# Shared raw-weight ring, earlier squares, kept weights and earlier output weights in a two-branch decoder layer

## The chip, the cores and the metric

The kernel runs on one core of one Trainium2 chip. The metric is the device time of one execution in microseconds (us). The instructions of one profiled execution are known with their start, duration and waits; all views shown are of that execution.

## The reference

One decoder layer over 2048 tokens of width 1024, with 16 meta tokens ahead of them. A root-mean-square norm is followed by one projection to 6400 columns; two attention branches run on its parts; their outputs are gated, projected, merged and projected once more, and a final norm follows.

```python
xn = rms_norm(h, norm_gain[l])
proj = xn @ w_in[l]
sb_q, sb_k, sb_v, sw_q, sw_k, sw_v, sb_z, sw_z, g_sb, g_sw = jnp.split(proj, offsets, axis=-1)
o_sb = stick_breaking_attention(sb_q, sb_k, sb_v, valid)       # 8 heads of 64, all earlier keys
o_sw = sliding_window_sink_attention(rope(sw_q), rope(sw_k), sw_v, attn_sinks[l], valid)  # 16 heads, 2 kv heads, window 128
y_sb = (o_sb * jax.nn.silu(sb_z)) @ w_branch_sb[l]
y_sw = (o_sw * jax.nn.silu(sw_z)) @ w_branch_swa[l]
merged = jax.nn.sigmoid(g_sb) * y_sb + jax.nn.sigmoid(g_sw) * y_sw
h = h + merged @ w_out[l]
return rms_norm(h, final_norm_gain)[:, BLOCK:]
```

Stick-breaking attention takes, for each query, a running product over the keys behind it; sliding-window attention ("banded" below) is a softmax over a band of 128 keys and one learned sink logit per head.

## The kernel before

The 2048 tokens stand in reverse order and are worked on in four groups of 512 (g = 0 to 3), two groups at a time: half 0 takes groups 2 and 3, half 1 takes groups 0 and 1. Matrix products keep nearly full single precision by splitting each operand into a high and a low part and running three matmuls for one (lines 376 to 378, and 211 to 213 and 268 to 270 at the end).

**Stages.** The start loads x, computes the norm's scales of the first group (`scales`: 8 loads of 128 x 512, a Square with a running sum on ScalarE for each, then a logarithm and an exponential for the inverse root) and `prep` builds xh and xl, the normalised input in two parts. Then in each half: projections for stick-breaking and the sliding window with `window` and `attend` (banded attention, lines 543 to 721) woven between them; after that the gate projections with `stick` (lines 724 to 854) woven between them. `finish` (lines 191 to 312) runs the branch projections, the merge, the output projection and the final norm, again half by half.

**Order.** TensorE's instructions stand in the order in which the program writes them, and `weave` mixes the two streams of work by a cost ratio. The other engines' orders come from a scheduler that places every instruction by a simulated timeline: among instructions that are ready it takes the one earliest in the program, so loads are drawn far ahead of the place where they are written, and work of a later stage is put among that of an earlier one. Each engine then works strictly in that order. All transfers are issued on SyncE's queue (line 55), also in one order. Buffers come from rings: a tile of a tag waits until one of the tag's buffers is free.

**Weights.** `weights` (line 156) loads one column tile of 128 columns as `raw` (512 KB, two buffers), splits it into `wh` and `wl` (three buffers each; the high part on GpSimd or ScalarE, the low part on GpSimd or VectorE) and stores both parts to HBM. The next call for the same tile takes them from HBM and forgets that they are there: the entry of `kept` is popped. Most column tiles are asked for twice, once in each half. The eight query tiles of the sliding window (`sw_q`) are asked for four times, since each half asks once for each of its groups.

**Turned tiles of v.** For stick-breaking, `sb_v` takes differences of neighbouring rows of v, turns them by TensorE transposes into `ps_zm` (one bank) and evacuates them with a split into `vt` (one buffer, 512 KB), which is stored to HBM as `vd` (lines 475 to 481). Each projection of v gives two such tiles, one for each group, turned while the next projection tile runs.

**Scales of half 1.** `group_scales` for groups 0 and 1 is called in the stick-breaking stage of half 0, between the tenth and the eleventh of its gate tiles (line 915). The 16 squares and the two inverse roots are ScalarE work; the results are used by `prep` at the end of half 0 and the start of half 1.

**Output projection.** For each group and each pair of row tiles (t0, t0 + 1), `finish` runs four blocks of 24 matmuls: the left half-row (ch = 0) for both row tiles, then the right one (ch = 1). Behind each block, VectorE adds the residual tile `res` (line 272) and ScalarE squares the sum (line 276). The output weights of ch = 0 are split during the merge (line 252), and those of ch = 1 (eight loads into the ring "a" of six, a cast on ScalarE, line 222, and a subtraction on VectorE, line 223, each) behind the first two blocks (line 282).

Of the kernel before, what the change touches and what calls it, by code (L numbers as in the profile page):

```python
# [7 lines left out]
F32 = mybir.dt.float32  # L8
F32R = mybir.dt.float32r
# [7 lines left out]
P = 128  # L17
D = 1024
# [26 lines left out]
def tile_kernel(ctx, tc, x, xt, meta, metat, gain, w_in, w_sb, w_sw, w_out, sinks, fgain,  # L45
# [27 lines left out]
    def late_consts():  # L73
        for i in range(2):
            DMA(sel[:, i, :], sel_c)
        DMA(skb, sinks.to_broadcast([P, 16]))
# [79 lines left out]
    def weights(c0, w=w_in):  # L156

        n = w.shape[2]
        wh, wl = (wp.tile([P, KT, P], F32R, tag=t, name=t, bufs=3)[:, :n, :] for t in ("wh", "wl"))
        key = w.name, c0  # L160
        if key in kept:
            for t, k in zip((wh, wl), kept.pop(key)):
                DMA(t, k)
            return wh, wl
        raw = wp.tile([P, KT, P], F32, tag="raw", name="raw", bufs=2)[:, :n, :]
        DMA(raw, w[c0 // P])
        split(wh, wl, raw)
        kept[key] = [dram(f"{t}_{w.name}_{c0}", [P, n, P], F32R) for t in "hl"]
        for t, k in zip((wh, wl), kept[key]):
            DMA(k, t)  # L170
        return wh, wl
# [19 lines left out]
    def finish(ringl, osw, first):  # L191
# [23 lines left out]
        for half, groups in enumerate(halves):  # L215
            part, merged, wo = {}, {}, {}

            def out_weights(k, ch):
                raw = small("a", AB)
                DMA(raw, w_out[0, k * P:(k + 1) * P, ch * GT:(ch + 1) * GT])  # L220
                h, l = wo[k, ch] = ringr(), ringr()
                A.copy(h, raw)
                V.tensor_tensor(l, raw, f32(h), op=ALU.subtract)
# [29 lines left out]
            for g in groups:  # L253
                for t0 in range(0, 4, 2):
                    res, ssq = {}, {}
                    end = (half, g, t0) == (1, groups[1], 2)
                    for ch in range(2):
                        cs = slice(ch * GT, (ch + 1) * GT)
                        for t in (t0, t0 + 1):
                            row = g * GT + t * P  # L260
                            if ch == 0:
                                res[t] = cp.tile([P, D], F32, tag="xr", name="res", bufs=3)
                                DMA(res[t], x[row:row + P, :])
                            acc = bank()
                            ts = slice(t * P, (t + 1) * P)
                            for k in range(KT):
                                (mh, ml), (wh, wl) = merged[k, g], wo[k, ch]
                                T.matmul(acc, lhsT=mh[:, ts], rhs=wh, start=k == 0, stop=False)
                                T.matmul(acc, lhsT=mh[:, ts], rhs=wl, start=False, stop=False)
                                T.matmul(acc, lhsT=ml[:, ts], rhs=wh, start=False, stop=k == KT - 1)  # L270
                            r = res[t][:, cs]
                            V.tensor_tensor(r, acc, r, op=ALU.add)
                            sq = cp.tile([P, GT], mybir.dt.bfloat16, tag="a", name="sq", bufs=AB)
                            if ch == 0:
                                ssq[t] = cp.tile([P, 2], F32, tag="ssq", name="ssq2", bufs=4)
                            A.activation(sq, r, AF.Square, accum_out=ssq[t][:, ch:ch + 1])
                            if end and t == 3:
                                V.tensor_tensor(r, r, fg[:, cs], op=ALU.mult)
                                if ch == 0:
                                    s0 = cp.tile([P, 1], F32, tag="rs", name="rs2", bufs=4)  # L280
                                    V.tensor_scalar(s0, ssq[t][:, 0:1], 1.0 / D, EPS, op0=ALU.mult, op1=ALU.add)
                        if (g, t0, ch) == (groups[0], 0, 0):
                            for k in range(KT):
                                out_weights(k, 1)
                    for t in (t0, t0 + 1):
                        row = g * GT + t * P
                        if end and t == 3:
                            s1 = ssq[t][:, 1:2]
                            rs, u = (cp.tile([P, 1], F32, tag="rs", name="rs2", bufs=4) for _ in range(2))
                            A.activation(rs, s1, AF.Ln, bias=s0, scale=1.0 / D)  # L290
                            A.activation(rs, rs, AF.Exp, scale=-0.5)
                            V.tensor_scalar(u, s1, 1.0 / D, s0, op0=ALU.mult, op1=ALU.add)
                            V.scalar_tensor_tensor(u, rs, rs, u, op0=ALU.mult, op1=ALU.mult)
                            V.tensor_scalar(u, u, -0.5, 1.5, op0=ALU.mult, op1=ALU.add)
                            a, b = (res[t][:, ch * GT:(ch + 1) * GT] for ch in range(2))
                            A.activation(a, a, AF.Copy, scale=rs)
                            V.tensor_scalar(b, b, rs, u, op0=ALU.mult, op1=ALU.mult)
                            DMA(out[row:row + P, GT:], b)
                            A.activation(a, a, AF.Copy, scale=u)
                            DMA(out[row:row + P, :GT], a)  # L300
                            continue
                        V.tensor_tensor(ssq[t][:, 0:1], ssq[t][:, 0:1], ssq[t][:, 1:2], op=ALU.add)
                        rs = cp.tile([P, 1], F32, tag="rs", name="rs2", bufs=4)
                        rsqrt(rs, ssq[t][:, 0:1], cp)
                        for ch in range(2):
                            cs = slice(ch * GT, (ch + 1) * GT)
                            V.scalar_tensor_tensor(res[t][:, cs], res[t][:, cs], rs, fg[:, cs], op0=ALU.mult, op1=ALU.mult)
                        DMA(out[row:row + P, :], res[t])
                if half == 0:
                    g2 = halves[1][g - groups[0]]  # L310
                    osw2.update({(k, g2): gated(ow, zw, k, g2, ringl, lambda: small("a", AB)) for k in range(8)})
# [10 lines left out]
    def ring_x(dt=F32):  # L322
        return tp.tile([P, GT], dt, tag="xs", name="xs", bufs=XS)

    def scales(src, rows, n, mk=ring_x):

        ssq = tp.tile([P, 2, 4], F32, tag="ssq", name="ssq", bufs=2)
        for i in range(n):
            for f in range(2):
                t = mk()  # L330
                DMA(t[:rows], src[i * rows:(i + 1) * rows, f * GT:(f + 1) * GT])
                A.activation(t[:rows], t[:rows], AF.Square, accum_out=ssq[:rows, f, i:i + 1])
        V.tensor_tensor(ssq[:rows, 0, :n], ssq[:rows, 0, :n], ssq[:rows, 1, :n], op=ALU.add)
        rs = tp.tile([P, 4], F32, tag="rs", name="rs", bufs=2)
        rsqrt(rs[:rows, :n], ssq[:rows, 0, :n], tp)
        return rs

# [4 lines left out]
            T.transpose(acc[:, i * rows:(i + 1) * rows], rs[:rows, i:i + 1].to_broadcast([rows, P]), ident[:rows, :rows])  # L342
        return acc[:, :n * rows]

    def group_scales(g, mk=ring_x):
        return scales(x[g * GT:(g + 1) * GT, :], P, 4, mk)

    def prep(g, rs, mk=ring_x, pool=False, mid=lambda: None):

# [111 lines left out]
    def sb_v(p):  # L461

        def use(g, acc, ms):
# [11 lines left out]
            def rows():  # L475
                tr = ps("zm")
                for i in range(4):
                    T.transpose(tr[:, i * P:(i + 1) * P], d[:, i * P:(i + 1) * P], ident)
                vt = tp.tile([P, 4, 2, P], F32R, tag="vt", name="vt", bufs=1)
                evac_split(vt[:, :, :, 0:64], vt[:, :, :, 64:128], tr.rearrange("p (b a d) -> p b a d", b=4, a=2))  # L480
                DMA(vd[p][g].rearrange("a p b d -> p b a d"), vt)

# [393 lines left out]
    for half, groups in enumerate(halves):  # L876
        with tc.tile_pool(name=f"swa{half}", bufs=1, side="left") as sp:
# [14 lines left out]
            drain(by_group(ts, groups[1:]))  # L892
            if m:
                late_consts()
            sw_k, sw_v, sw_q, attend, ending = window(half, groups, sp)
            q = [[lambda p=p: sw_q(p) for p in (2 * s, 2 * s + 1)] for s in range(4)]
            steps = [(s, g) for s in range(4) for g in groups]
# [8 lines left out]
        with tc.tile_pool(name=f"sb{half}", bufs=1, side="left") as bp:  # L906
            vsplit[0] = False
            side = stick(groups, bp)
            drain(tiles_by_tile(gts[3:4], groups))
            rest = 25 if half == 0 else 23  # L910
            cost_sb = 8 * sum(4 * (4 - g) for g in groups) * 1.31 + 16 * 0.75
            ratio = cost_sb / ((rest - 4) * 10.4)
            left = weave(tiles_by_tile(gts[4:14], groups), side, ratio)
            if half == 0:
                rs0, rs1 = (group_scales(g) for g in halves[1])
            weave(tiles_by_tile(gts[14:rest], groups), side, ratio, left)
            drain(side)
        if half == 0:
            ts = [mk() for mk in gts[rest:]]
# [70 lines left out]
```

## Time and profile before

| | |
|---|---|
| runs | 5490.61, 2217.91, 2214.62 us; median 2217.91 us |
| profiled execution | 2214.4 us, span from first to last instruction 2212.7 us |
| TensorE (PE) busy | 2153.2 us, 97% of the span, 10614 matmuls |
| weight loads into TensorE (PEld) | 1768.0 us, 80% |
| VectorE (DVE) busy | 1353.8 us, 61% |
| ScalarE (ACT) busy | 1006.8 us, 46% |
| GpSimd (POOL) busy | 381.9 us, 17% |
| DMA | 382.48 MB, 173 GB/s on average |
| TensorE clock granted | 0.996 of full speed on average |

How to read the views: times are microseconds from the span's start unless marked otherwise. L376 is line 376 of the kernel. A tile name with an arrow, such as `vt<-ps_zm`, says what an instruction writes and reads. A bracket behind a row of the timeline gives the time that the engine stood idle before the instruction, and what released it. SPq is SyncE's queue of transfers. A list of waits gives, for each waiting line and the line waited for, the total, the number of times and the longest. A wait for several things is put down to the last of them.

### The profile page before, as it was taken

To read this page: it belongs to the slowest core of one execution; us is meant where nothing else is said; L and a number is where in the kernel's file an instruction comes from. 1 tells how busy PE (TensorE), PEld (TensorE's weight loads), DVE (VectorE), ACT (ScalarE), POOL (GpSimd) and SP (SyncE) were. 2 spreads that over 40 slices of the span, in tenths; PEclk is the share of its full clock that TensorE was granted. 3 is DMA by queue.
4 is the path that set the end of the run, shared out by engine and by line. 5 is a ranking of instruction groups with operands and counts; after the bars stand their busy time and mean duration, and the time that the engine had idled before them with its cause. 6 is when DMAs were issued, how large, how long until landed. Compare 5 with 4: busy or idle time off the path is not lost.

```text
span 2212.7 us, 30250 instructions
## 1 busy us (share of the span) xinstructions
PE 2153.2 (97%) x10614; PEld 1768.0 (80%) x10614; DVE 1353.8 (61%) x2105; ACT 1006.8 (46%) x2328; POOL 381.9 (17%) x494
## 2 busy tenths in 40 slices
PE   4999999999999999999999999999999999999998
PEld 3888887788888888788887888888888888787876
DVE  4578777356555433677655888787775436454443
ACT  4367777433333323667753555555553202221121
POOL 2123343322223201233310000000000232000000
PEclk9999999999999999999999999999999999999999
DMA  8654546946545465444446433333323986468422
GB/s 292 217 175 169 180 170 223 277 157 203 186 165 170 147 225 193 154 170 162 153 136 190 122 120 112 103 99 119 117 86 116 349 282 198 151 222 273 155 91 86
DMA packets 175384, 382.48 MB, mean 173 GB/s; under 512 B 22944, under 2 KB 41056, under 8 KB 175232
## 3 DMA queue, kind: packets, MB, share of 16 engines
q1 hardware_dynamic: 175232, 380.54, 51.0%
q8 instruction: 84, 1.38, 0.2%
q14 instruction: 68, 0.56, 0.1%
HBM read 231.04 MB, written 149.36 MB: 172 GB/s over the span
## 4 chain that ended last, share of the span: by engine, by line
PE 88%; DVE 3%; DMA 3%; ACT 3%; issue 3%; POOL 1%; SPq 0%; DVEq 0%; ACTq 0%; POOLq 0%
PE ps_g L376 15%; PE ps_g L377 15%; PE ps_g L378 15%; PE ps_o L827 6%; PE ps_z L779 6%; PE ps_t L801 5%; PE ps_z L642 2%; PE ps_o L688 2%; PE ps_g L212 1%; PE ps_g L213 1%; PE ps_z L213 1%; PE ps_z L211 1%; PE ps_g L211 1%; PE ps_z L212 1%; PE ps_t L213 1%
## 5 line engine op out<-in xcount | busy, mean ns | idle before, releaser
L376 PE MATMUL ps_g<-xh,wh 128*128 128x512 f32 x1600 | 660.8, 413 | 4.3 <-DVE tmp L566 2.4
L377 PE MATMUL ps_g<-xl,wh 128*128 128x512 f32 x1600 | 630.1, 394 | 3.9 <-DVE xl L362 3.9
L378 PE MATMUL ps_g<-xh,wl 128*128 128x512 f32 x1600 | 629.8, 394 | 0.0
L790 DVE TENSOR_TENSOR_SCAN row<-row 128x512 f32<-128x512 f32 (+2 forms) x320 | 372.7, 1167 | 176.4 <-POOL row L788 101.4
L378 PEld LDWEIGHTS ps_g<-xh,wl 128*128 128x128 f32 x1600 | 301.7, 189 | 67.7
L376 PEld LDWEIGHTS ps_g<-xh,wh 128*128 128x128 f32 x1600 | 303.1, 189 | 54.1 <-DVE tmp L566 3.2
L377 PEld LDWEIGHTS ps_g<-xl,wh 128*128 128x128 f32 x1600 | 303.4, 190 | 49.4 <-DVE xl L362 4.4
L783 ACT ACTIVATE row<-ps_z 128x512 f32<-128x512 f32 (+1 forms) x320 | 172.0, 538 | 276.3 <-PE ps_z L779 228.6
L113 DVE SCALAR_TENSOR_TENSOR wtl<-ps_t,wth 128x512 fp32r<-128x512 f32 (+1 forms) x320 | 190.0, 594 | 42.8 <-ACT wth L112 41.3
L112 ACT ACTIVATE wth<-ps_t 128x512 fp32r<-128x512 f32 (+1 forms) x320 | 170.4, 532 | 97.2 <-PE ps_t L801 95.6
L779 PE MATMUL ps_z<-kt,q 128*128 128x512 f32 (+3 forms) x640 | 185.0, 369 | 0.3 <-ACT row L783 0.3
L801 PE MATMUL ps_t<-ident,row 128*128 128x128 f32 x1088 | 171.6, 273 | 1.2 <-DVE row L790 1.2
L801 PEld LDWEIGHTS ps_t<-ident,row 128*128 128x128 f32 x1088 | 135.9, 140 | 37.3 <-DVE row L790 1.7
L788 POOL TENSOR_SCALAR_AFFINE_SELECT row<-row 128x128 f32<-128x128 f32 x128 | 44.2, 346 | 619.0 <-ACT row L783 553.4
L108 POOL TENSOR_SCALAR wh<-raw 128x1024 fp32r<-128x1024 f32 (+1 forms) x71 | 74.1, 1044 | 423.8 <-PE ps_g L377 337.3
L779 PEld LDWEIGHTS ps_z<-kt,q 128*128 128x128 f32 x640 | 118.7, 188 | 26.5 <-ACT row L783 0.8
L827 PE MATMUL ps_o<-wth,vc 128*128 128x512 f32 (+1 forms) x320 | 125.7, 393 | 1.3 <-DVE tmp L832 1.1
L518 ACT ACTIVATE tmp<-ps_g 128x512 f32<-128x512 f32 x112 | 67.1, 599 | 121.7 <-PE ps_g L378 112.6
L650 ACT ACTIVATE sc<-sc,nm 128x129 f32<-128x129 f32 x256 | 100.0, 393 | 37.3 <-DVE nm L648 36.8
L827 PE MATMUL ps_o<-wtl,vc 128*128 128x512 f32 (+1 forms) x320 | 116.8, 365 | 0.0
L109 POOL TENSOR_TENSOR wl<-raw,wh 128x1024 fp32r<-128x1024 f32 (+1 forms) x44 | 98.0, 2228 | 19.0 <-ACT wh L106 16.1
L250 ACT CAST ringl<-gt 128x512 fp32r<-128x512 f32 x32 | 19.9, 621 | 130.1 <-DVE gt L248 128.1
(232 smaller groups left out, 3333.9 us busy)
## 6 DMA issues: line engine op xcount, KB each, us to landing
raw<-in_w_in SPq DMA_DIRECT2D x58, 512.0 KB, 4.3
h_in_w_in<-wh SPq DMA_DIRECT2D x58, 512.0 KB, 3.2
l_in_w_in<-wl SPq DMA_DIRECT2D x58, 512.0 KB, 3.6
wh<-h_in_w_in SPq DMA_DIRECT2D x58, 512.0 KB, 3.6
wl<-l_in_w_in SPq DMA_DIRECT2D x58, 512.0 KB, 4.8
q<-qd SPq DMA_DIRECT2D x128, 128.0 KB, 3.3
vc<-vd SPq DMA_DIRECT2D x48, 256.0 KB, 2.9
qd<-tmp SPq DMA_DIRECT2D x32, 256.0 KB, 2.2
```

The source lines that it names most:

```text
L109: (V if vsplit[0] else G).tensor_tensor(l, src, f32(h), op=ALU.subtract)
L112: A.activation(h, acc, AF.Copy, scale=scale)
L113: V.scalar_tensor_tensor(l, acc, scale, f32(h), op0=ALU.mult, op1=ALU.subtract)
L376: T.matmul(acc, lhsT=wh[:, k, :], rhs=xh[g][:, k, :], start=k == 0, stop=False)
L377: T.matmul(acc, lhsT=wh[:, k, :], rhs=xl[g][:, k, :], start=False, stop=False)
L378: T.matmul(acc, lhsT=wl[:, k, :], rhs=xh[g][:, k, :], start=False, stop=k == KT - 1)
L650: A.activation(sc[:, hh, :], sc[:, hh, :], AF.Exp, bias=nm[:, hh:hh + 1], accum_out=den[:, hh:hh + 1])
L779: T.matmul(z[:, :w], lhsT=lq, rhs=kt[h][:, k0:k0 + w], start=t == 0, stop=t == 1)
L783: A.activation(r[:, :w], z[:, :w], AF.Sigmoid, scale=-1.0)
L790: V.tensor_tensor_scan(r[:, :w], r[:, :w], r[:, :w], last[j] if n else 1.0, op0=ALU.mult, op1=ALU.min)
L801: T.transpose(tr[:, j * P:(j + 1) * P], rows_of[h, g, n - (j > i), j][:, k0:k0 + P], ident)
L827: T.matmul(o[:, :n], lhsT=v, rhs=r, start=first and r is wh, stop=last and r is wl)
```

## The change

1. **Ring of raw weights.** `raw` gets three buffers instead of two. The turned tiles `vt` (one buffer of their own before) and the residual tiles `res` of the output stage (three buffers of their own before) now come from the same ring.
2. **Kept weights stay kept.** The entry of `kept` is read and no longer popped, so a tile that was stored once is never loaded raw and split again. This concerns the eight `sw_q` tiles in half 1; all others are asked for twice only.
3. **Scales of half 1.** The two `group_scales` calls move from the stick-breaking stage of half 0 to the place before `window` in half 0, ahead of banded attention. Their results get a tag of their own. The two `weave` calls around the old place become one with the same order.
4. **Output weights of ch = 1.** They are issued behind the first block (t = 0) rather than behind the second (t = 1).

```diff
-            for t, k in zip((wh, wl), kept.pop(key)):
+            for t, k in zip((wh, wl), kept[key]):
                 DMA(t, k)
             return wh, wl
-        raw = wp.tile([P, KT, P], F32, tag="raw", name="raw", bufs=2)[:, :n, :]
+        raw = wp.tile([P, KT, P], F32, tag="raw", name="raw", bufs=3)[:, :n, :]
...
-                                res[t] = cp.tile([P, D], F32, tag="xr", name="res", bufs=3)
+                                res[t] = wp.tile([P, KT, P], F32, tag="raw", name="res", bufs=3).rearrange("p k c -> p (k c)")
...
                             A.activation(sq, r, AF.Square, accum_out=ssq[t][:, ch:ch + 1])
+                            if (g, t, ch) == (groups[0], 0, 0):
+                                for k in range(KT):
+                                    out_weights(k, 1)
...
-                        if (g, t0, ch) == (groups[0], 0, 0):
-                            for k in range(KT):
-                                out_weights(k, 1)
...
-        rs = tp.tile([P, 4], F32, tag="rs", name="rs", bufs=2)
+        rs = tp.tile([P, 4], F32, tag=tag, name="rs", bufs=2)
...
-                vt = tp.tile([P, 4, 2, P], F32R, tag="vt", name="vt", bufs=1)
+                vt = wp.tile([P, 4, 2, P], F32R, tag="raw", name="vt", bufs=3)
...
             if m:
                 late_consts()
+                rs0, rs1 = (group_scales(g, tag="later") for g in halves[1])
             sw_k, sw_v, sw_q, attend, ending = window(half, groups, sp)
...
-            left = weave(tiles_by_tile(gts[4:14], groups), side, ratio)
-            if half == 0:
-                rs0, rs1 = (group_scales(g) for g in halves[1])
-            weave(tiles_by_tile(gts[14:rest], groups), side, ratio, left)
+            weave(tiles_by_tile(gts[4:rest], groups), side, ratio)
```

More of the change, by code (lines that the diff above doesn't have):

```diff
@@ L323, in ring_x, with scales @@
         return tp.tile([P, GT], dt, tag="xs", name="xs", bufs=XS)
-    def scales(src, rows, n, mk=ring_x):
+    def scales(src, rows, n, mk=ring_x, tag="rs"):
         ssq = tp.tile([P, 2, 4], F32, tag="ssq", name="ssq", bufs=2)
@@ L343, in spread, with group_scales @@
         return acc[:, :n * rows]
-    def group_scales(g, mk=ring_x):
-        return scales(x[g * GT:(g + 1) * GT, :], P, 4, mk)
+    def group_scales(g, mk=ring_x, tag="rs"):
+        return scales(x[g * GT:(g + 1) * GT, :], P, 4, mk, tag)
     def prep(g, rs, mk=ring_x, pool=False, mid=lambda: None):
```

## The prediction

> **What bounds the kernel now.** I read the page first, then the waits of TensorE, then a table of stages, then the timeline at each place where TensorE stood still. Of the page, the span, the busy times and the chain that ended last:
>
> ```profile
> span 2212.7 us, 30250 instructions
> PE 2153.2 (97%) x10614; PEld 1768.0 (80%) x10614; DVE 1353.8 (61%) x2105; ACT 1006.8 (46%) x2328; POOL 381.9 (17%) x494
> ...
> PE 88%; DVE 3%; DMA 3%; ACT 3%; issue 3%; POOL 1%; SPq 0%; DVEq 0%; ACTq 0%; POOLq 0%
> ```
>
> TensorE is busy for all but 2212.7 - 2153.2 = 59.5 us, and the change neither adds nor removes a matmul. So everything it can bring is a share of these 59.5 us (plus slow-clock time, below), and everything it can cost is new idle time there. About 2% is what a measurement of this kernel can tell from no change: 0.02 x 2214.4 = 44 us, three quarters of all idle time. The waits that the change touches, from the list of TensorE's waits over the whole span (columns: total us, times, longest):
>
> ```profile
> PE ps_t L342 <- DVE rs L124: 7.1, 1, 7.1
> PE ps_z L268 <- ACT ringr L222: 4.2, 2, 2.1
> ...
> PE ps_zm L486 <- DVE vt L113: 2.7, 2, 1.6
> ...
> PE ps_z L269 <- DVE ringr L223: 0.7, 3, 0.2
> ```
>
> And the table of stretches, where PEclk is the granted clock:
>
> ```profile
> core 0: us, PE busy (x) PEld busy (x) DVE busy (x) ACT busy (x) POOL busy (x), PEclk, DMA share, GB/s
> 40.00:48.00 8.00, 0.53 (x3) 0.43 (x4) 2.06 (x10) 2.52 (x8) 0.00 (x0) 0.70 1.05 400
> 55.00:111.00 56.00, 56.00 (x285) 46.03 (x284) 28.29 (x45) 22.45 (x47) 9.68 (x9) 1.00 0.61 216
> ...
> 394.80:398.20 3.40, 2.88 (x7) 2.30 (x8) 1.28 (x3) 2.57 (x5) 2.81 (x2) 0.50 0.93 313
> 913.60:917.00 3.40, 3.40 (x12) 2.60 (x13) 3.40 (x7) 1.44 (x3) 1.59 (x1) 0.50 0.02 5
> ...
> 1896.70:1900.10 3.40, 2.71 (x11) 2.00 (x12) 2.96 (x5) 3.05 (x6) 0.00 (x0) 1.00 0.57 162
> ```
>
> Two short stretches ran at half the clock, each right behind a TensorE gap. At half clock half of the busy time is lost: 2.88 / 2 = 1.4 us and 3.40 / 2 = 1.7 us.
>
> **Output weights a block sooner.** Around the first output block of half 0 (timeline of SyncE's queue, ScalarE and TensorE; start, duration):
>
> ```profile
> 1888.67 10.12 SPq L55 DMA_DIRECT2D a<-in_w_out  x8
> 1895.88 0.63 ACT L276 ACTIVATE sq<-res 128x512 bf16<-128x512 f32 x1 [4.88 <-DVE res L272]
> 1896.51 3.24 ACT L222 CAST ringr<-a 128x512 fp32r<-128x512 f32 x6
> 1897.16 0.49 PE L268 MATMUL ps_z<-ringr,ringl 128*128 128x512 f32 x1 [2.10 <-ACT ringr L222]
> ```
>
> The weights were requested at 1888.67, but ScalarE takes its work in order: it sat 4.88 us waiting for block t = 1 to end, did that block's square, and only then cast the weights that t = 0 of the second half-row needs. With the casts ahead of that square, this 4.88 us of ScalarE idle time takes them. The same eight loads, casts and VectorE subtractions are issued, so nothing is added; what is late next is the square, for which nobody waits within a block. Both halves do it (the wait is listed twice): 4.2 + 0.7 = 4.9 us off. Bounds 0 to -4.9; I take -4.9, as the data lag is all that would be left.
>
> **Squares of the next half.** The waits of TensorE between 350 and 404 us, where banded attention of half 0 ends, then four groups of ScalarE (total us, mean ns):
>
> ```profile
> PE ps_o L688 <- DVE os L694: 2.3, 1, 2.3
> PE ps_o L688 <- ACT ph L112: 1.6, 1, 1.6
> PE ps_o L688 <- POOL cl L675: 1.0, 2, 0.8
> PE ps_o L688 <- DVE pl L113: 0.5, 2, 0.3
> ```
> ```profile
> L332 ACT ACTIVATE xs<-xs 128x512 f32<-128x512 f32 (+1 forms) x26 | 16.3, 627 | 6.1 <-DMA xs<-in_x 6.0
> ...
> L518 ACT ACT_TABLE_LOAD x5 | 6.4, 1283 | 0.1
> ...
> L118 ACT ACT_TABLE_LOAD x2 | 2.6, 1283 | 0.8 <-DVE ssq L117 0.8
> L119 ACT ACT_TABLE_LOAD x2 | 2.6, 1283 | 0.0
> ```
>
> The program puts the two group_scales calls into stick-breaking, but the scheduler drew them forward into the last units of banded attention, among sigmoid gates. Each logarithm and each exponential of the inverse root then reloads the function table (4 loads), and the gates load theirs back (2 of the five of L518): six loads, 7.7 us of ScalarE, where attention's softmax chain has no slack. The sum of the four waits is 5.4 us. Half 1 has the same end without squares; its TensorE waits from 880 to 1165 us are
>
> ```profile
> PE ps_g L376 <- DVE tmp L566: 2.2, 1, 2.2
> PE ps_o L688 <- DVE os L694: 0.9, 1, 0.9
> PE ps_o L688 <- DVE pl L113: 0.2, 1, 0.2
> ```
>
> so about 1.1 us should remain: -4.3 us, and the half-clock stretch at 394.8 with it, -1.4. Bounds 0 and -5.4 - 1.4 = -6.8.
>
> At the new place, before window(), 16 loads of 256 KB pass on SyncE's queue and 16 squares of 627 ns (10 us) on ScalarE, between 55 and 111 us. There TensorE is never idle, ScalarE is busy 22.45 of 56 us, the DMA engines 0.61; 4.2 MB more over 56 us are 75 GB/s on 216. The table there is still the logarithm's, so none is loaded. Behind a square that waits for its load stand the evacuations of projection tiles; two ps_g banks cover one late tile. The squares' waits so far are 6.1 us for 26, so 16 x 0.23 = 3.7 us at most if none were covered: bounds 0 to +3.7, I take +1.0, nearer to the covered end since TensorE's row shows no idle time at all.
>
> **Turned tiles in the raw ring.** A turned tile has one buffer now, so the next evacuation waits in ScalarE's queue for the store (the landing is the last column of the DMA row):
>
> ```profile
> vd<-vt SPq DMA_DIRECT2D x16, 512.0 KB, 4.3
> ...
> 899.51 0.60 ACT L112 ACTIVATE vt<-ps_zm 128x512 fp32r<-128x512 f32 x1 [6.20 <-DMA vd<-vt]
> ```
>
> With three slots the second tile of a pair waits for no store. The two waits of L486 for vt (2.7 us) go: bounds 0 and -2.7, I take -2.7. And at 899.51 ScalarE lost 6.20 us ahead of the rotary copies for which, some ten us later, TensorE waited 2.2 us (L376 <- L566 above); 6.2 is more than 2.2, so I take all of it and its half-clock stretch: -2.2 - 1.7 = -3.9, bounds 0 and -3.9.
>
> **Raw weights with three slots.** At the start the DMA engines move 400 GB/s without a pause, and TensorE's 7.1 us wait ends with the last square of the second group, whose load was issued behind a raw load:
>
> ```profile
> 37.04 0.95 SPq L55 DMA_DIRECT2D raw<-in_w_in  x1
> 38.08 0.97 SPq L55 DMA_DIRECT2D xs<-in_x  x1
> ```
>
> A third slot lets one more 512 KB load in early: 0.5 MB / 400 GB/s = 1.3 us later for what is behind it, or 1.3 us sooner if this raw load has gone ahead by then; a longer gap may hold the clock down once more (1.7). Bounds -1.3 to +3.0, I take +1.3.
>
> **Kept weights and residual tiles.**
>
> ```profile
> raw<-in_w_in SPq DMA_DIRECT2D x58, 512.0 KB, 4.3
> ...
> res<-in_x SPq DMA_DIRECT2D x16, 512.0 KB, 4.0
> ...
> L108 POOL TENSOR_SCALAR wh<-raw 128x1024 fp32r<-128x1024 f32 (+1 forms) x71 | 74.1, 1044 | 423.8 <-PE ps_g L377 337.3
> ...
> L109 DVE TENSOR_TENSOR wl<-raw,wh 128x1024 fp32r<-128x1024 f32 x30 | 37.4, 1247 | 6.8 <-POOL wh L108 6.7
> ```
>
> w_in has 50 column tiles; 58 raw loads show that the 8 sliding-window query tiles were split again in half 1. That goes: 8 x 1.044 = 8.4 us of GpSimd, 8 x 1.247 = 10 us of VectorE, 16 stores less, 8 raw loads become 16 kept ones. All of it lies beside matmuls that run through 880 to 1165 us with 3.3 us of idle time, counted above: 0. The residual loads now queue behind the last raw tiles of w_sb; those are split blocks before the first residual is added: 0, at worst one landing, 4.0 us.
>
> **The sum**, against the profiled execution's 2214.4 us (span 2212.7 and 1.7 around it; 3.5 below the median of the runs, 2217.91, and at the lowest, 2214.62): -4.9 - 4.3 - 1.4 + 1.0 - 2.7 - 3.9 + 1.3 = -14.9, so **2199.5 us**. With every bound at its best end: -4.9 - 6.8 - 2.7 - 3.9 - 1.3 = -19.6, 2194.8; I let the likeliest case run from 2195 to 2206.
>
> [...] The trace has it both ways: half clock behind gaps of 2.2 us or less at 394.8 and 913.6, full clock behind the 2.10 us gap at 1897.
>
> **Rivals.** (1) The gaps that hang on the scheduler's order come back elsewhere: it places all instructions anew, so the waits for vt and for L566 need not vanish. Then only output weights and squares count: -4.9 - 4.3 - 1.4 + 2.3 = -8.3, 2206.1. For it: such waits are small and many; against: both have a store as their first cause. (2) The change does not do what it says for the output weights: the casts stay late because ring "a" has six buffers for eight loads. Then 4.9 is lost: 2204.4. Against it: the six casts ran in one piece, their data long there. (3) The half-clock stretches do not come from short gaps and stay: 3.1 us less, 2202.6; the full clock at 1897 speaks for it, that both stretches stand behind gaps against it. [...] (4) **Slower**: the shared ring makes weights late. A turned tile holds a raw slot in program order; if the first raw tile behind a pair had to wait for the pair's second store, the worst place is
>
> ```profile
> 168.41 0.59 SPq L55 DMA_DIRECT2D vd<-vt  x1
> ...
> 161.89 0.40 PE L376 MATMUL ps_g<-xh,wh 128*128 128x512 f32 x1
> ```
>
> The second row opens the tile of query weights 3, whose raw tile comes next in the ring. Store, load and split would be done at 168.41 + 4.3 + 4.3 + 1.0 + 1.2 = 179.2, so TensorE waits 17.3 us, and again behind the other three pairs of half 0, with more slack; at half the price for these, 17.3 x 2.5 = 43 us, -14.9 + 43 = +28, 2242.5. It decides from a total of 15 us on. Against it: three slots hold a pair and one raw tile, so the raw tile needs only the split of the raw tile before it, and that runs as soon as TensorE gives a wh buffer back, three weights ahead.
>
> **How the numbers follow.** Forecast 0.50; (1) 0.23; (2) 0.06; (3) 0.08; (4) 0.09; something unseen that costs over 44 us 0.03, other 0.01. The range runs from 2192, a little below the best of all bounds, to 2224, past rivals 1 to 3 and into the smaller versions of 4 (one place, or one landing of 4.0 and the 3.7 and 3.0 of the bounds on top of 2206.1). Faster by over 2% would need 44 of 59.5 us: 0.01. Slower by over 2% is the tail of 4 and the unseen: 0.05. Within: 0.94.
>
> **What would show it.** Right: raw loads x50 and wl splits on VectorE x22; no table load at L118 or L119; L268 <- ACT L222 gone from TensorE's waits; no wait of vt for its own store; squares between 55 and 111 us; half clock at the start only. Wrong: a TensorE wait for wh or wl, L376 waiting for L354 or L361 longer than now, or idle time of TensorE above 59.5 us.

## The result, and the profile after

The changed kernel takes 2219.86 us (median of 20 runs) where the kernel before takes 2217.05 us (20 runs): a ratio of 1.0018, 95% interval 1.0012 to 1.0025. Two of the 20 runs before (5490.61 and 2385.12 us) were slow ones that the ratio leaves out; the median of the other 18 is 2215.70 us, so the loss is 4.2 us. Forecast were 2199.5 us. The time lies inside the range of 2192 to 2224 and within 2% of before, but it moved the other way: some 15 us of gain were expected and 4 us of loss came.

The page of the profiled execution (2219.1 us) after the change:

```profile
span 2217.4 us, 30189 instructions
...
PE 2155.0 (97%) x10614; PEld 1770.1 (80%) x10614; DVE 1351.3 (61%) x2097; ACT 999.3 (45%) x2322; POOL 375.9 (17%) x486
...
raw<-in_w_in SPq DMA_DIRECT2D x50, 512.0 KB, 5.4
```

TensorE is idle for 2217.4 - 2155.0 = 62.4 us, against 59.5 before. The work that should go has gone: 50 raw loads, 61 instructions fewer. What TensorE waits for (us in total, times, longest):

```profile
...
PE ps_t L342 <- DVE rs L124: 8.1, 1, 8.1
PE ps_g L376 <- POOL wh L108: 5.5, 1, 5.5
PE ps_o L688 <- DVE os L694: 5.3, 2, 4.4
...
PE ps_z L642 <- DVE sc L646: 3.7, 3, 1.6
PE ps_g L376 <- DVE tmp L566: 2.6, 2, 2.2
...
PE ps_g L378 <- DVE wl L109: 1.1, 1, 1.1
```

The waits of L268 for the casts and of L486 for vt are no longer listed. In their place stand waits for weights (`wh`, `wl`), which the list of before did not have at all. So most of the prediction's signs of being right came (50 raw loads, no table load at L118 or L119, no wait for the casts or for vt), but so did two signs of being wrong, a wait for wh or wl and idle time above 59.5 us, and half clock did not stay at the start only. The start and the stretches behind the new gaps, with the granted clock (PEclk) as the third number from the end:

```profile
core 0: us, PE busy (x) PEld busy (x) DVE busy (x) ACT busy (x) POOL busy (x), PEclk, DMA share, GB/s
40.00:48.00 8.00, 0.32 (x3) 0.13 (x1) 1.80 (x6) 4.31 (x14) 0.00 (x0) 0.69 1.03 366
55.00:111.00 56.00, 53.25 (x261) 42.32 (x260) 29.74 (x55) 30.99 (x77) 9.90 (x8) 0.97 0.70 251
90.60:94.20 3.60, 3.60 (x10) 2.79 (x10) 2.37 (x4) 3.47 (x9) 2.48 (x3) 0.53 0.44 176
172.70:179.50 6.80, 4.49 (x10) 3.12 (x11) 5.55 (x5) 1.24 (x2) 3.53 (x3) 0.50 0.95 342
398.00:404.80 6.80, 6.01 (x16) 4.87 (x17) 2.84 (x6) 1.64 (x3) 1.87 (x3) 0.50 0.89 355
```

Between 55 and 111 us TensorE was busy all the time before; now 2.75 us are missing and the clock is 0.97. The last two stretches, at half clock, lie at the wait for wh and at the end of banded attention in half 0.

**Where in the run.** All these kernels issue the same 10,614 matmuls in the same order, so the k-th matmul of one trace can be set against the k-th of another. Its start minus that of before, counted from the first matmul, is the lag; the table has what the lag gains in each stretch of the kernel before (us; negative is time won). Its left column is the changed kernel; the other columns belong to the experiments below.

| stretch of before | changed | squares alone | output weights alone | ring alone | without ring | v by `tmp`, raw 3 | v by `tmp`, raw 2 |
|---|---|---|---|---|---|---|---|
| start to 60 | 0.4 | -1.3 | -1.0 | 1.1 | -0.5 | -0.3 | -0.2 |
| 60 to 110 | 5.5 | 5.0 | 0.3 | 0.0 | 3.5 | 6.3 | 4.8 |
| 110 to 190 | 7.7 | -0.1 | 0.0 | 9.4 | 0.0 | -1.6 | -1.4 |
| 190 to 350 | 1.8 | 0.1 | 0.0 | 1.7 | 0.1 | 0.1 | 0.1 |
| 350 to 420 | -1.1 | -7.7 | -1.2 | -1.7 | -7.6 | -7.5 | -7.5 |
| 420 to 890 | -0.1 | 0.0 | 0.0 | 0.0 | -0.1 | -0.1 | -0.1 |
| 890 to 960 | -2.6 | 0.5 | -0.1 | 11.5 | 0.3 | -2.7 | -2.7 |
| 960 to 1880 | 0.1 | 0.1 | 0.0 | 0.7 | 0.1 | 0.1 | 0.5 |
| 1880 to the end | -7.0 | 0.6 | -5.3 | 1.7 | -6.0 | -6.0 | -6.9 |

Each column is one profiled execution. In "output weights alone" every engine works in the same order as before up to 1860 us, and still the table has -1.0 at the start and -1.2 between 350 and 420: two executions of one order differ by that much, so a single cell of about 1 us shows nothing.

The changed kernel loses 15 us between 60 and 350 us and wins back 11 later. The place of the largest loss, on TensorE and on SyncE's queue (two views; start, duration, and the idle time ahead in the bracket):

```profile
173.91 0.80 PE L376 MATMUL ps_g<-xh,wh 128*128 128x512 f32 x1 [5.52 <-POOL wh L108]
176.23 0.80 PE L378 MATMUL ps_g<-xh,wl 128*128 128x512 f32 x1 [1.10 <-DVE wl L109]
```
```profile
132.77 0.62 SPq L55 DMA_DIRECT2D vd<-vt  x1
133.45 4.72 SPq L55 DMA_DIRECT2D raw<-in_w_in  x2
138.25 0.59 SPq L55 DMA_DIRECT2D vd<-vt  x1
...
167.00 0.63 SPq L55 DMA_DIRECT2D vd<-vt  x1
167.68 3.62 SPq L55 DMA_DIRECT2D raw<-in_w_in  x2
171.39 0.59 SPq L55 DMA_DIRECT2D vd<-vt  x1
```

Here the raw loads go out two at a time, directly behind the store of a pair's first turned tile. In the kernel before the raw loads do not hang on these stores:

```profile
125.66 0.43 SPq L55 DMA_DIRECT2D raw<-in_w_in  x1
126.72 0.62 SPq L55 DMA_DIRECT2D vd<-vt  x1
...
155.72 0.42 SPq L55 DMA_DIRECT2D raw<-in_w_in  x1
160.47 0.63 SPq L55 DMA_DIRECT2D vd<-vt  x1
```

Counted from the start, the eleventh raw load carries query weights 3 in both kernels: it goes out at 125.66 us before and at 167.68 us after. And the waits of SyncE's queue between 95 and 140 us, after the change:

```profile
SPq L55 <- DVE vt L113: 15.6, 1, 15.6
SPq L55 <- PE ps_g L378: 7.2, 2, 4.8
...
SPq L55 <- DMA vd<-vt: 3.6, 1, 3.6
```

The queue stood still for 15.6 us ahead of the first store of vt, with the raw loads behind that store. The second raw load then waited 3.6 us more, until that store had landed: it takes the turned tile's slot. The first one was not late for want of slots. The splits on GpSimd and VectorE, timeline of the changed kernel:

```profile
105.06 1.05 POOL L108 TENSOR_SCALAR wh<-raw 128x1024 fp32r<-128x1024 f32 x1 [7.51 <-PE ps_g L377]
...
139.16 1.40 POOL L108 TENSOR_SCALAR wh<-raw 128x1024 fp32r<-128x1024 f32 x1 [16.37 <-issue]
```

The raw tile split at 105 us was the last one loaded (its low part ended at 107.4), and the first turned tile is written at 131.4. For 24 us all three slots were empty, and no load was issued.

The end of banded attention in half 0 is late for the same reason (timeline of GpSimd, VectorE, ScalarE and TensorE):

```profile
388.84 1.05 POOL L108 TENSOR_SCALAR wh<-raw 128x1024 fp32r<-128x1024 f32 x1 [3.32 <-DMA raw<-in_w_in]
389.92 1.63 DVE L109 TENSOR_TENSOR wl<-raw,wh 128x1024 fp32r<-128x1024 f32 x1 [2.19 <-POOL wh L108]
393.67 0.41 ACT L650 ACTIVATE sc<-sc,nm 128x129 f32<-128x129 f32 x1 [5.26 <-DVE nm L648]
398.79 0.76 PE L688 MATMUL ps_o<-ph,vv 128*128 128x512 f32 x1 [4.43 <-DVE os L694]
```

The split waits for a late raw load, VectorE waits for the split, and the softmax work that stands behind it in VectorE's order comes late to ScalarE and to TensorE.

### The profile page after: what moved, and what is told of

Its sections match the earlier page's. It is cut to its first block, busy times and chain, and to the rows that moved or that the text cites. A ratio compares the mean times of both kernels' runs of the same rounds, so it can differ in the third digit from the quotient of the medians.

```text
span 2217.4 us, 30189 instructions
## 1 busy us (share of the span) xinstructions
PE 2155.0 (97%) x10614; PEld 1770.1 (80%) x10614; DVE 1351.3 (61%) x2097; ACT 999.3 (45%) x2322; POOL 375.9 (17%) x486
## 4 chain that ended last, share of the span: by engine, by line
PE 89%; DVE 3%; DMA 3%; issue 2%; ACT 2%; POOL 0%; SPq 0%; ACTq 0%; POOLq 0%; DVEq 0%
PE ps_g L376 15%; PE ps_g L378 15%; PE ps_g L377 15%; PE ps_o L827 6%; PE ps_z L779 6%; PE ps_t L801 5%; PE ps_o L688 3%; PE ps_z L642 2%; PE ps_g L213 1%; PE ps_g L212 1%; PE ps_z L213 1%; PE ps_z L211 1%; PE ps_g L211 1%; PE ps_z L212 1%; PE ps_t L213 1%
## 5 line engine op out<-in xcount | busy, mean ns | idle before, releaser
L108 POOL TENSOR_SCALAR wh<-raw 128x1024 fp32r<-128x1024 f32 (+1 forms) x63 | 67.5, 1072 | 374.3 <-PE ps_g L377 248.8
L568 POOL TENSOR_TENSOR tmp<-tmp 128x512 f32<-128x512 f32 (+1 forms) x37 | 48.1, 1301 | 197.5 <-DVE tmp L567 157.6
```

## The experiments

Three theories stood against each other. **A**: a ring's slots are handed out in the order in which the program writes the tiles, so a raw load written behind a turned pair is not issued before the pair has its slots, that is, before it is evacuated. **B**: the earlier squares hold up everything behind them, the weights too. **C**: any edit makes the scheduler place all work anew, and a few us move at random. All ratios below are to the kernel before, run beside it on the same chip.

**1. The whole change without its shared ring.**

```diff
-        raw = wp.tile([P, KT, P], F32, tag="raw", name="raw", bufs=3)[:, :n, :]
+        raw = wp.tile([P, KT, P], F32, tag="raw", name="raw", bufs=2)[:, :n, :]
-    res[t] = wp.tile([P, KT, P], F32, tag="raw", name="res", bufs=3).rearrange("p k c -> p (k c)")
+    res[t] = cp.tile([P, D], F32, tag="xr", name="res", bufs=3)
-                vt = wp.tile([P, 4, 2, P], F32R, tag="raw", name="vt", bufs=3)
+                vt = tp.tile([P, 4, 2, P], F32R, tag="vt", name="vt", bufs=1)
```

> The whole change without its shared ring: turned tiles, raw weights (two buffers) and residual tiles each have the ring of before; kept weights, earlier squares and earlier output weights stay as in the changed kernel. Theory A (a raw load written behind a pair of turned tiles cannot be issued before the pair has its slots): the waits of L376 for wh (5.5 us) and of L378 for wl (1.1 us) at 174 to 177 us vanish with the half clock behind them (about 2.5 us), the store waits of vt come back (L486, 2.7 us), so about 2217.05 - 5.7 (output weights) - 4.9 (end of attention of half 0) + 3.7 (gap near 90 us) = 2210, ratio to before about 0.997. Theory B (the earlier squares, 16 loads of 256 KB on SyncE's queue and 16 squares on ScalarE between 63 and 97 us, put everything behind them off, the weights too): the wait for wh stays, and with the waits for vt back it takes 2220 to 2223. Theory C (any new order moves a few us about): anywhere from 2210 to 2222, with gaps at other places than before.

Measured: 2203.67 against 2213.84 us, ratio 0.9955 (0.9943 to 0.9968); that is below theory A's 0.997 because attention's end won 7.6 us where 4.9 were expected. TensorE's waits between 120 and 200 us:

```profile
PE ps_zm L486 <- DVE vt L113: 2.7, 2, 1.7
PE ps_t L502 <- DVE tmp L471: 0.4, 1, 0.4
```

The waits for wh and wl are gone, those for vt are back. From 110 to 350 us and from 420 to 1880 us no stretch of the table differs from before by more than 0.3 us, which speaks against C; and kept weights, which act in half 1, move nothing there. The squares are as early as in the changed kernel, so B falls as the cause of the late weights.

**2. The shared ring alone** (the three edits above, the other way round, on the kernel before).

> The kernel before with the shared ring alone: turned tiles and residual tiles in the ring of raw weights, with three slots. Theory A: SyncE's queue has no raw load between the load behind one turned tile's store and the next pair's store, TensorE waits for wh or wl of query weights 3 near 165 to 175 us (5 to 9 us with half clock), and bunched splits delay the end of attention in half 0; with -2.7 (vt) and -3.9 (the gap at 911 us) against it, 2217.05 + 9.2 + 1.8 + 1.5 - 6.6 = about 2223, ratio 1.001 to 1.005. Theory B: no wait for wh; the gains of the ring alone remain, 2217.05 - 6.6 = about 2210. Theory C: a few us either way, without a wait for wh near 170 us.

Measured: 2238.63 us, ratio 1.0113 (1.0099 to 1.0127): 25 us, four times what theory A expected. The wait at query weights 3 is there without any early squares (120 to 200 us):

```profile
PE ps_g L376 <- POOL wh L108: 4.7, 1, 4.7
...
PE ps_g L378 <- DVE wl L109: 1.1, 1, 1.1
```

The surprise is half 1, 880 to 1170 us:

```profile
PE ps_g L378 <- DVE wl L109: 8.9, 2, 4.9
PE ps_o L688 <- DVE os L694: 0.9, 1, 0.9
PE ps_g L376 <- POOL wh L108: 0.7, 1, 0.7
```

In this kernel half 1 splits the sliding-window query tiles once more, needs raw slots for them and waits behind the pairs there too (9.6 us of waits and the slow clock behind them, less what is won near 911 us: 11.5 us in the table). Behind the wait that ends at 936.60 us matmuls of 128x512 started 0.42 to 0.43 us apart (937.19 to 941.03 us), and 0.22 to 0.24 between 943.41 and 944.57 us.

**3. The earlier squares alone** (`group_scales` ahead of `window`, its own tag, one undivided weave).

> The kernel before with the earlier squares alone. Theory A: the gap near 90 us (L376 waits for the evacuation at L566, 2.2 us, and half clock behind it: 3.7 us together) is the squares' own price, the table loads among the gates of half 0 go, and with them 4.9 us of attention's end: about 2217.05 + 3.7 - 4.9 = 2216, same within 2 us, and no wait for wh. Theory B: the squares delay the weights: a wait of L376 for wh near 170 us and 2224 to 2228. Theory C: 2212 to 2222.

Measured: 2211.17 us, ratio 0.9989 (0.9980 to 0.9998). No wait for weights. The row of the squares, and ScalarE and TensorE around the gap near 87 us (three views):

```profile
L332 ACT ACTIVATE xs<-xs 128x512 f32<-128x512 f32 (+1 forms) x26 | 16.3, 627 | 16.9 <-DMA xs<-in_x 16.9
```
```profile
82.97 0.63 ACT L332 ACTIVATE xs<-xs 128x512 f32<-128x512 f32 x1 [3.92 <-DMA xs<-in_x]
...
83.64 0.63 ACT L332 ACTIVATE xs<-xs 128x512 f32<-128x512 f32 x1
...
84.55 0.58 ACT L564 ACTIVATE tmp<-ps_g 32x512 f32<-32x512 f32 x1
```
```profile
87.80 0.77 PE L376 MATMUL ps_g<-xh,wh 128*128 128x512 f32 x1 [1.67 <-DVE tmp L566]
```

ScalarE waits 3.92 us for a load, does two squares, and only then the four rotary copies (L564, L565) that free a projection bank. The table gives the squares' price as 5.0 us between 60 and 110 us, and their gain at attention's end as 7.7.

**4. Earlier output weights alone.**

> The kernel before with the output weights a block sooner alone. All theories: the waits of L268 and L269 for the casts of L222 go (4.9 us in the trace of before), and nothing before 1880 us changes if the scheduler keeps its order there: 2217.05 - 5.7 = 2211.4, ratio 0.9974. Theory C (any edit reorders the rest): up to 3 us beside that, with differences before 1880 us.

Measured: 2207.90 us, ratio 0.9973 (0.9964 to 0.9982), as forecast; the table shows 5.3 us behind 1880 and, ahead of it, no more than the scatter between two executions of one order.

**5. Order or number of slots.** The changed kernel with all its slots; only `weights` of the next column tile is called one tile ahead, from the first query tiles to the end of the main sequence of banded attention.

```diff
+    def ahead(items, after=None):
+        for (mk, gr, meta), nxt in zip(items, [i[0] for i in items[1:]] + [after]):
+            w, use, wants = made.pop() if made else mk()
+            if nxt is not None:
+                made.append(nxt())
...
-            main = chain(*[chain(tiles_by_tile(q[s], [g]), tiles_by_tile(sbt[3 + j:4 + j], groups, m))
+            main = ahead(items)
```

> The changed kernel with its shared ring, but in the main sequence of banded attention the weights of each column tile are written one tile ahead, so that its raw load stands in front of the turned pair in the ring's order and not behind it. Same slots, same loads, same stores. Theory A (the order in which slots are handed out): the raw load no longer waits for the pair's evacuation; the waits for wh and wl at 168 to 177 us (with half clock 9.2 us), the waits of L642 at 149 and 291 us (3.6 us) and the late end of attention in half 0 (3.8 us) go: 16.6 us off the changed kernel, ratio to the kernel before about 1.0018 - 0.0075 = 0.994. Theory D (three slots are too few, or the turned tile's store is too slow, whatever the order): a wait for wh or wl of 3 us or more stays near 170 us and the ratio is 0.999 or above.

Measured: 2212.48 against 2214.83 us, ratio 0.9991 (0.9982 to 0.9999). The wait for wh near 170 us is gone (9.2 us of lag at that one place in the changed kernel). The load of query weights 3, still the eleventh, now goes out ahead of the second pair, whose first store starts at 168.76 us:

```profile
143.32 0.38 SPq L55 DMA_DIRECT2D raw<-in_w_in  x1
```

Order alone has done this: slots, loads and stores are the same. But by the ratios (1.0018 - 0.9991) only some 6 of the 16.6 us that A expected came, and the ratio is one that theory D allowed. The waits of SyncE's queue from 95 to 140 us:

```profile
SPq L55 <- DVE vt L113: 15.6, 1, 15.6
SPq L55 <- PE ps_g L378: 8.1, 2, 4.8
```

The first pair still stands ahead of its raw loads. Behind that projection of v come two query tiles whose weights are kept, so the next raw tile is three tiles on, and one tile ahead does not lift it over the pair. The waits of banded attention near 151 and 287 us and its late end (3.2 us) stayed.

**6. The ring with kept weights.**

```diff
-            for t, k in zip((wh, wl), kept.pop(key)):
+            for t, k in zip((wh, wl), kept[key]):
```

> The kernel before with the shared ring and with kept weights that stay kept, without the two other parts. Theory A: in half 1 the query weights need no raw slot any more, so the two waits of L378 for wl at 932 and 947 us (6.7 + 6.5 us with half clock) go, and those of half 0 stay: ratio 1.0113 - 0.006 = 1.005. Rival (kept weights are worth nothing in any company, as the prediction had it): ratio 1.010 to 1.012, and the two waits stay.

Measured: 2222.78 us, ratio 1.0038 (1.0025 to 1.0050). Both waits of half 1 are gone. So kept weights are worth some 16 us beside the ring and, by experiment 1, nothing without it: the same edit has two prices.

**7 and 8. The squares a little later** (written behind the sliding-window keys and values), on experiment 1 and on experiment 5.

> The whole change without its shared ring, as in the first run, with the squares written a little later: behind the tiles of the sliding-window keys and values, ahead of the first query tiles. Theory E (the gaps of 85 to 95 us come from evacuations of sliding-window key tiles that stand behind squares in ScalarE's order): they go, 2.5 us off the first run, ratio 0.9955 - 0.001 = 0.9944. Rival (a square that waits for its load delays whatever projection stands behind it): a like gap turns up between 100 and 140 us, and the ratio stays at 0.995 to 0.997.

> The changed kernel with both: weights written one tile ahead in the shared ring, and squares behind the sliding-window keys and values. Theories A and E: the shared ring's own gains (vt waits 2.7 us, the gap near 911 us with its clock 2.5 to 3.9 us) come on top, and the gap near 90 us goes: 0.994 - 0.0017 = about 0.992. Theory D: 0.997 or above.

Measured: 0.9947 (0.9934 to 0.9961) and 0.9984 (0.9974 to 0.9994). Neither tells theory E from its rival. In experiment 7 the squares ran from 59.3 to 94.5 us, nearly the stretch where they had been in experiment 1 (59.8 to 88.2), and TensorE's wait for the evacuation at L566 stayed (1.67 us at 86.8 us). Moving a line hardly moved the work. Experiment 8 missed the 0.992 of theory A and lies where theory D had it: as in experiment 5, the first pair still stands ahead of its raw loads.

**9 and 10. Turned tiles through the ring of temporaries.** Each goes as two halves, one per head, with three raw slots and seven temporaries (9) or with two raw slots and nine temporaries (10).

```diff
-                vt = wp.tile([P, 4, 2, P], F32R, tag="raw", name="vt", bufs=3)
-                evac_split(vt[:, :, :, 0:64], vt[:, :, :, 64:128], tr.rearrange("p (b a d) -> p b a d", b=4, a=2))
-                DMA(vd[p][g].rearrange("a p b d -> p b a d"), vt)
+                for a in range(2):
+                    vt = tmp(F32R).rearrange("p (b d) -> p b d", b=4)
+                    evac_split(vt[:, :, 0:64], vt[:, :, 64:128],
+                               tr.rearrange("p (b a d) -> p b a d", b=4, a=2)[:, :, a, :])
+                    DMA(vd[p][g][a], vt)
```

> The changed kernel with its three raw slots, shared by raw weights and residual tiles, but with the turned tiles taken out of it: each goes as two halves (one per head, 256 KB) through the ring of temporaries with its seven buffers, which is freed by other things than raw loads. Theory A (the turned pair in the ring's order is what costs): no wait for wh or wl near 170 us, no bunched splits at 149 us, attention's end in half 0 as in the first run, and the vt waits gone as well (2.7 us, and the gap near 905 us with its clock 2.5 us): ratio 0.9955 - 0.002 = 0.993 to 0.994. Theory F (the third slot and the residual tiles in the ring are what costs): 0.998 or above, with late raw loads in half 0.

> As the run before in the turned tiles (two halves through the ring of temporaries), but with two raw buffers and residual tiles in their own ring as in the kernel before; the 4 KB per partition that are freed give the ring of temporaries nine buffers. Theory A: 0.993 to 0.994, within 1 us of the run with three raw slots, since raw loads are early in both. Theory F: faster than that run by 5 us or more. A rival to both: halves of turned tiles that wait for their stores hold temporaries back, and the evacuations of rotary tiles wait for one: 0.996 or above.

Measured: 2202.38 us, ratio 0.9949 (0.9937 to 0.9961), and 2199.69 us, ratio 0.9940 (0.9928 to 0.9952), against 2213.18 us. Experiment 9 differs from the changed kernel in the turned tiles alone, and SyncE's queue from 95 to 140 us waits for the splits of raw tiles, as it did in the kernel before (15.3 us there):

```profile
SPq L55 <- POOL wh L108: 12.9, 2, 12.5
SPq L55 <- PE ps_g L378: 7.0, 2, 4.8
```

The load of query weights 3 goes out at 106.5 us here. So theory F, with 0.998 or above, falls: it is the turned tiles in the ring, not the third slot and not the residual tiles. Experiment 10 is the fastest of all, 13 us ahead of the kernel before; its lead of 2.7 us over 9 is no clear difference, since the two intervals overlap.

## Why the prediction was wrong

**The step that failed** is the argument against rival 4: "three slots hold a pair and one raw tile, so the raw tile needs only the split of the raw tile before it". It counted slots and took for granted that a load goes out as soon as a slot is empty. The slots were empty for 24 us and no load went out. What decided was the order in the ring: raw tiles are written when their column tile begins, turned tiles some matmuls later, and a raw tile written behind a pair goes out behind the store of the pair's first tile, the next raw tile when that store has landed. That order within the ring is the cause is shown by experiments 2, 5 and 9. That the second raw load takes the slot of a turned tile is seen in its wait for the store; that the first is held back by the scheduler's handing out of slots in written order is inferred from the empty slots, and no view shows it.

In size: 14.9 us of gain were forecast and the span grew by 4.7 us (2217.4 - 2212.7), a difference of 19.6. Of these, 12.2 us lie between 110 and 350 us (9.5 lost, 2.7 of gain forecast), where experiments without turned tiles in the ring lose nothing; 4.6 at attention's end, where the ring again is the cause; and 4.5 at the squares' new place. The rest, -1.7, is small.

**Rival 4** (0.09) had mechanism and place right: query weights 3. Its price was too high there, 17.3 us, because it let the raw load wait until the pair's second store had landed; the load went out right behind the first store, and the place cost 9.2 us with its half clock. Such a smaller version of rival 4 is what the upper end of the range was drawn for, so that the time lies inside it is not luck alone. It foresaw a turn of the sign from 15 us on. Experiment 1 against the changed kernel gives the ring's price within the whole, its own gains taken off: 1.0018 - 0.9955 = 0.63%, 14 us, and the sign turned by a hair.

The other terms:

- *Output weights*, -4.9: 5.3 us by the lag and 5.9 by the runs. Right; rival 2 falls.
- *The squares' old place*, -4.3 - 1.4 = -5.7: 7.7 in experiment 3, some 1 us of it perhaps scatter. Right in kind. In the changed kernel only 1.1 is left, no more than the ring alone shows with the squares at their old place (1.7): late raw loads delay splits, and these attention's last units (the four rows at 389 to 399 us above).
- *The squares' new place*, +1.0: 5.0 in experiment 3, above its bound of 3.7. "TensorE's row shows no idle time" is no measure of slack: the loads, now among raw loads and prep's, let the squares wait 16.9 us instead of 6.1, and two projection banks did not cover 3.9 us in one piece.
- *Turned tiles*, -2.7 and -3.9: the waits for vt went where the weights were in time (110 to 190 us: -1.4 to -1.6), and -2.6 came near 911 us. Right in kind, by a third or more too large, since part of the gaps turns up again as smaller waits.
- *Third slot at the start*, +1.3: the L342 wait went from 7.1 to 8.1 us in the changed kernel, but it is 5.6 to 7.2 us in the runs with two slots and 6.6 to 8.1 in those with three. The direction fits, the size can't be told from scatter.
- *Kept weights*, 0: right alone, wrong in company. Costing each edit beside the kernel before missed that the ring makes the second split expensive (experiment 6).
- *Half clock behind short gaps* (against rival 3): in experiment 3 the clock was 0.55 behind a wait of 2.10 us and 1.00 behind one of 2.09 us, see below.
- *What a measurement can tell*, 2% or 44 us: far too wide. The intervals here reach 0.06 to 0.14%, 1 to 3 us, to either side.

With the turned tiles elsewhere the rest of the sum holds fairly well: experiment 9 wins 11 us where 14.9 were forecast, and most of the difference is the squares' new place. Partly that is luck: by the table the squares' new place costs 6.3 us instead of 1.0 and the turned tiles win 4.3 instead of 6.6, but the squares' old place wins 7.5 instead of 5.7 and the output weights 6.0 instead of 4.9.

## What to carry to other kernels

Count not only the slots of a shared ring but the order in which its users are written: a load that is to run ahead must not stand behind a tile that waits for a computation, however many slots are empty. An idle engine row is no proof of cover; look at the longest single wait that the moved work would put ahead of an evacuation, and set it against the banks. And price the parts of a change in company as well as alone: kept weights were worth 0 or 16 us.

## What the runs showed of the hardware

A wait of the same length was followed by a lower clock at one place and not at another. In experiment 3 the same line waits 2.10 us at 1893 us and 2.09 us at 2123 us:

```profile
1893.10:1896.10 3.00, 2.78 (x7) 1.98 (x8) 3.00 (x6) 2.58 (x5) 0.00 (x0) 0.55 0.66 199
2122.90:2125.90 3.00, 2.77 (x11) 2.04 (x12) 3.00 (x6) 2.55 (x5) 0.00 (x0) 1.00 0.70 210
```

The granted clock behind the first is 0.55, with 7 matmuls in 3 us, and behind the second 1.00, with 11. Matmuls of 128x512 started 0.42 to 0.43 us apart between 1894.36 and 1896.49 us, and 0.23 to 0.24 us apart between 2123.86 and 2126.90 us.

The kernel before had a clock of 0.50 for 3.40 us (913.60 to 917.00) behind a wait of 2.20 us, and of 1.00 behind the one of 2.10 us at 1897. From these numbers, as an estimate: a gap of 2 us in this kernel is priced at its length plus 0 to 1.7 us, half of the 3.40. What decides between the two was not shown.
